# A decoder layer on one core: the sample's state taken up after a group's convolution, stores by ScalarE's queue, keys in four tiles, values in strips

## The chip, the core and the metric

The kernel runs on one core of a Trainium2 chip. The time is that of one launch on the device, in microseconds (us); lower is better. TensorE (PE) multiplies matrices, VectorE (DVE) and ScalarE (ACT) work on tiles, GpSimd (POOL) does a few small things here, and transfers are issued on the queues of SyncE (SP), POOL and ScalarE. Each engine, and each queue, takes its instructions strictly in order.

## What is computed

One step of a hybrid decoder layer for a prompt of 256 tokens and, with the same weights, 8 samples of one token each. All 264 columns go through every projection together. In short:

```python
h = rmsnorm(x) * norm_mix
q, k, v, z, xbc, dt, qm, gates = split(h @ w_in)
A = swa(q, k, v)               # window 128, 16 heads, sinks; samples see cache_swa_k/v
B = ssd(conv(xbc), z, dt)      # 4 groups of 8 heads; samples update state_ssm, state_conv
M = mem_attend(qm, k_mem, v_mem)   # 256 tokens: from mem_prompt, or cache_mem_k/v for samples
x = x + (sig(gA)*(A@w_up_swa) + sig(gB)*(B@w_up_ssd) + sig(gM)*(M@w_up_mem)) @ w_out
x = x + (silu(h2 @ w_gate) * (h2 @ w_up)) @ w_down      # h2 = rmsnorm(x)
```

Outputs are x of both kinds, the new keys and values, the SSD states and the last rows of the convolution. Of the sample's state, `s_ssm` (8 x 32 x 64 x 128 floats), every number is read, decayed, added to and written back.

## The kernel before

**Weights.** Every product is made in three matmuls of a 128x128 weight block (high part times high part, high times low, low times high). The weights stream in units: a unit is 512 KB, loaded on SP's queue into one of four `raw` tiles, split by ScalarE into `hi` (line 181) and by DVE into `lo` (line 182), up to three units ahead, and used by PE in 24 matmuls of 264 columns (line 160). Units are listed by hand in the order of the work: 32 for the keys and values of the memory (`pmem`), then those of `w_in` in groups of 8 units (`pin`), the three up projections (`pua`, `pum`, `pus`), `pout`, and the feed-forward part (`pg`, `pu`, `pdn`). A group ends with an `after` that empties four PSUM tiles; there are five PSUM tiles for this, so the next group starts as they come free.

**Side work.** All else is written as Python generators that are stepped once after each unit. `Side` holds a list of tasks and a credit: each unit adds 1.0 (list `side`) or 0.75 (list `slow`), a `yield n` spends n, and a `yield None` sets the credit to zero, that is, ends the step. A task may name what has to be ready first. In list `side` stand the norm of the memory (`mem_norm`), x's norm (`prep_x`), constants, the prompt's memory attention (`mem_prompt_work`), the window attention (`swa_keys`, `swa`), and per group of the SSD the convolution (V), the chunks (X) and the norm (N). In list `slow` stand the samples' memory attention, keys (`mem_sample_work`) and values (`mem_sample_values`), and the samples' state (`ssd_sample_work`, Y). The position in the program that comes out of this is a wish: a planner inside the framework, with a model of the times, fixes the order of each engine's instructions at build time.

**Start.** SP's queue loads the first quarters of `mem_prompt`, two small vectors into `vg` (lines 205, 206), then the first raw unit. PE turns `mem_prompt` into features (`mem_feats`, lines 308 to 318), three pairs ahead of the first unit's matmuls. ScalarE squares `mem_prompt` for its norm at line 327.

**Values of the memory for samples** (lines 726 to 749). For each sample and each half of the tokens: a tile of 1024 values, four matmuls (one for each head) of 256 columns into the four strips of 32 PSUM rows, with weights that are zero but for one column. Keys and values come through `ahead`, which keeps `depth` loads going, into two `lm` tiles.

**State of the samples** (lines 1280 to 1298). 32 pieces of four samples and two heads each. A piece is loaded on POOL's queue (line 591) into one of four slots of `ring`; ScalarE multiplies it four times (line 1294), DVE adds and reduces it (lines 1295, 1296), and POOL's queue stores it (line 1297). `ssd_sample_work(g)` may begin when `ssd_chunk_work(g)` has ended (line 1246).

**Stores.** Results go out on POOL's queue, those that ScalarE writes last too: om (line 691), v_tok (787), the last rows of the convolution (1047, 1049), so (1206) and sg (1399).

Of the kernel before, what the change touches and what calls it, by code (L numbers as in the profile page):

```python
# [77 lines left out]
def tile_hybrid_decoder_step(  # L78
# [80 lines left out]
    def mm(out, lhsT, rhs, start=True, stop=True):  # L159
        nc.tensor.matmul(out, lhsT=lhsT, rhs=rhs, start=start, stop=stop)  # L160
# [18 lines left out]
    def split(hi, lo, src):  # L179

        act(hi, src, AF.Copy)  # L181
        V.tensor_tensor(lo, src, hi.bitcast(F32), op=ALU.subtract)  # L182

# [18 lines left out]

    for t in range(2):
        load_mem(t, 0, 0)
    nc.sync.dma_start(vg[0:16], norm_mem[0].rearrange("(c p) -> c p", p=P))
    nc.sync.dma_start(vg[16:32], norm_mix[0].rearrange("(c p) -> c p", p=P))
# [45 lines left out]
    def do_split(n):  # L252
# [10 lines left out]
        else:  # L263
            split(hi, lo, raw)
# [8 lines left out]
    def group(name, loads, nk, xh, xl, after, perm=False, before=None):  # L273
# [145 lines left out]
    def prep_x():  # L419
# [4 lines left out]
        for h in range(2):  # L424
            for t in range(2):
# [3 lines left out]
                yield 1.3  # L429
# [129 lines left out]
    def h_group(col, after, perm=False, before=None):  # L559
        group("pin", w_loads(w_in[0], col), KT, hh, hl, after, perm, before)  # L560
# [34 lines left out]
    mem_loads = ahead([(None, c[0, b, mc * P:(mc + 1) * P].rearrange("m h d -> m (h d)"))  # L595
                       for c in (cache_mem_k, cache_mem_v) for b in range(NS) for mc in range(2)], lm, 2)
# [3 lines left out]
                         for j in range(16) for b in (0, 4)], lambda _: piece(512), 4)  # L600


    def mem_prompt_work():
# [50 lines left out]
        for hp in range(2):  # L654
            den = tiny("den", 4)
            pT = [t2("pT").rearrange("p (mc t) -> p mc t", mc=2) for _ in range(2)]
            for tb in range(2):
# [15 lines left out]
                for h in range(2):  # L673
                    V.tensor_scalar(pm[:, h], pm[:, h], den[:, 2 * tb + h:2 * tb + h + 1], None, op0=ALU.mult)
                p2 = sps("pmT").rearrange("p (h mc t) -> p h mc t", h=2, mc=2)
# [5 lines left out]
                yield 2.2  # L681
            for h in range(2):
# [8 lines left out]
                nc.gpsimd.dma_start(m_d[:, 2 * hd:2 * hd + 2, 0:NP], om)  # L691
                yield 0.2
        slow.ready.add("q")
    def mem_sample_work():
# [3 lines left out]
        for b in range(NS):  # L698
            qb = t4("qb")[:, 0:1024]
            nc.gpsimd.dma_start(qb, qd[b:b + 1].broadcast_to([P, 1024]))  # L700
            for mc in range(2):
                kc = next(mem_loads)
# [23 lines left out]
    def mem_sample_values():  # L726
        pT = mT["p"]
# [12 lines left out]
        o = t1("omsb")[:, 0:256]  # L740
        V.tensor_copy(o, po[:, 0:256])
        ps = sps("omT")
        for d in range(2):
            tr(ps[:, d * P:(d + 1) * P], o[:, d * P:(d + 1) * P])
        o = tiny("omsT", 64)
        V.tensor_copy(o.rearrange("p (h d b) -> p d h b", h=4, d=2),
                      ps[:, 0:256].rearrange("p (d h e) -> p d h e", d=2, h=4)[:, :, :, 0:NS])
# [23 lines left out]
    def swa_keys():  # L771
# [15 lines left out]
        nc.gpsimd.dma_start(p_swa_v[0, 0].rearrange("t h d -> t (h d)"), v_tok[:, 1])  # L787
# [33 lines left out]
    def swa():  # L821
# [37 lines left out]
        for a in range(2):  # L859
# [6 lines left out]
            yield 1.0  # L866
# [809 lines left out]
```

## Time and profile before

| What | us |
| --- | --- |
| Median of three runs | 1933.8 |
| Lowest and highest run | 1928.26, 1938.96 |
| The profiled execution | 1933.54 |
| Its span, first to last instruction | 1931.8 |
| PE busy | 1905.2 (99%) |
| DVE busy | 1168.0 (60%) |
| ACT busy | 969.7 (50%) |

PE's busy time counts any moment in which a matmul is in the array. A matmul of 264 columns is in it for some 285 ns, while the next starts 0.12 us after it, so a busy PE can still have lost a little at each change between kinds of matmul; only its idle time is a wait. The other engines' busy time matters where PE waits for one of them.

### The profile page before, as it was taken

Reading aid. Unit: us, or ns where it says so; the run is one execution under the profiler, and the core shown is the slowest. Engines: PE = TensorE matmul, PEld = TensorE weight load, DVE = VectorE, ACT = ScalarE, POOL = GpSimd, SP = SyncE. Lnnn points to the kernel's source line nnn. Section 1 sums busy time; section 2 is a strip of 40 time slices with the busy share of each in tenths; the row PEclk is TensorE's granted clock in tenths of the full one; section 3 lists DMA queues with packets and bytes.
Section 4 is the critical chain, followed back from the end, with each engine's and each line's share of the span. In section 5 each row is a group of like instructions: output and inputs, shape, how many; then the busy total and the mean of one; then the engine's idle time right before and its main releaser. Section 6 shows DMA issues by size and latency. Waiting matters only on the chain.

```text
span 1931.8 us, 37682 instructions
## 1 busy us (share of the span) xinstructions
PE 1905.2 (99%) x15401; PEld 1857.1 (96%) x15401; DVE 1168.0 (60%) x2246; ACT 969.7 (50%) x1423; POOL 133.6 (7%) x269
## 2 busy tenths in 40 slices
PE   8999999999999999999999999999999999999998
PEld 6899999989999999999999999999999999999998
DVE  5665577665568878588455666555445555445553
ACT  6654456665657685646444444444334434334443
POOL 3010101001002122011000000000000000000000
PEclk9999999999999999999999999999999999999999
DMA  8686758767668789778656656665556665566653
GB/s 278 209 264 214 212 171 297 223 190 234 200 181 279 241 228 301 250 262 282 180 189 213 222 182 176 184 182 180 183 178 183 178 185 177 184 177 183 176 192 126
DMA packets 191956, 402.92 MB, mean 209 GB/s; under 512 B 13891, under 2 KB 16242, under 8 KB 191648
## 3 DMA queue, kind: packets, MB, share of 16 engines
q1 hardware_dynamic: 169856, 324.13, 54.6%
q0 software_dynamic: 21776, 76.33, 11.9%
q8 instruction: 120, 1.97, 0.4%
q14 instruction: 52, 0.43, 0.1%
q10 hardware_dynamic: 152, 0.07, 0.0%
HBM read 376.53 MB, written 26.22 MB: 208 GB/s over the span
## 4 chain that ended last, share of the span: by engine, by line
PE 87%; DMA 4%; issue 4%; DVE 3%; ACT 2%; POOL 1%; ACTq 0%; SPq 0%; POOLq 0%; DVEq 0%
PE pin L160 25%; PE pu L160 13%; PE pdn L160 13%; PE pg L160 13%; PE pus L160 5%; PE pout L160 5%; PE pmem L160 5%; DMA ring<-in_state_ssm_dram 2%; PE pum L160 1%; PE pua L160 1%; DVE lo L182 1%; DMA ld<-in_cache_mem_v_dram 1%; DVE ring L1295 1%; DMA ld<-in_cache_mem_k_dram 1%; ACT hi L181 0%
## 5 line engine op out<-in xcount | busy, mean ns | idle before, releaser
L182 DVE TENSOR_TENSOR lo<-raw,hi 128x1024 fp32r<-128x1024 f32 (+1 forms) x626 | 746.8, 1196 | 599.4 <-ACT hi L181 598.2
L181 ACT ACTIVATE hi<-raw 128x1024 fp32r<-128x1024 f32 (+1 forms) x626 | 646.0, 1036 | 835.0 <-PE pin L160 191.8
L160 PE MATMUL pin<-hh,hi 128*128 128x264 f32 x1728 | 489.3, 287 | 0.6 <-DVE sig L1439 0.5
L160 PE MATMUL pin<-hl,hi 128*128 128x264 f32 x1728 | 489.0, 286 | 0.0
L160 PE MATMUL pin<-hh,lo 128*128 128x264 f32 x1728 | 473.8, 285 | 1.8 <-DVE lo L182 1.8
L160 PEld LDWEIGHTS pin<-hh,hi 128*128 128x128 f32 x1728 | 325.4, 189 | 5.6 <-issue 3.6
L160 PEld LDWEIGHTS pin<-hl,hi 128*128 128x128 f32 x1728 | 325.5, 188 | 2.7 <-issue 2.4
L160 PEld LDWEIGHTS pin<-hh,lo 128*128 128x128 f32 x1728 | 317.3, 188 | 3.8 <-DVE lo L182 2.3
L160 PE MATMUL pdn<-fah,hi 128*128 128x264 f32 x704 | 199.7, 285 | 0.0
L160 PE MATMUL pdn<-fal,hi 128*128 128x264 f32 x704 | 199.4, 285 | 0.0
L160 PE MATMUL pu<-h2h,hi 128*128 128x264 f32 x704 | 199.4, 284 | 0.0
L160 PE MATMUL pu<-h2l,hi 128*128 128x264 f32 x704 | 199.3, 284 | 0.0
L160 PE MATMUL pg<-h2l,hi 128*128 128x264 f32 x704 | 199.1, 285 | 0.0
L160 PE MATMUL pg<-h2h,hi 128*128 128x264 f32 x704 | 198.4, 284 | 0.0
L160 PE MATMUL pdn<-fah,lo 128*128 128x264 f32 x704 | 197.0, 284 | 0.0
L160 PE MATMUL pu<-h2h,lo 128*128 128x264 f32 x704 | 196.6, 284 | 0.0
L160 PE MATMUL pg<-h2h,lo 128*128 128x264 f32 x704 | 196.1, 284 | 0.0
L160 PEld LDWEIGHTS pdn<-fah,hi 128*128 128x128 f32 x704 | 132.7, 189 | 0.1
L160 PEld LDWEIGHTS pu<-h2h,hi 128*128 128x128 f32 x704 | 132.7, 189 | 0.0
L160 PEld LDWEIGHTS pg<-h2h,hi 128*128 128x128 f32 x704 | 132.7, 188 | 0.0
L160 PEld LDWEIGHTS pdn<-fal,hi 128*128 128x128 f32 x704 | 132.6, 188 | 0.1
L160 PEld LDWEIGHTS pu<-h2l,hi 128*128 128x128 f32 x704 | 132.6, 188 | 0.0
(531 smaller groups left out, 2966.0 us busy)
## 6 DMA issues: line engine op xcount, KB each, us to landing
raw<-in_w_in_dram SPq DMA_DIRECT2D x218, 512.0 KB, 4.3
raw<-in_w_gate_dram SPq DMA_DIRECT2D x88, 512.0 KB, 3.7
raw<-in_w_up_dram SPq DMA_DIRECT2D x88, 512.0 KB, 3.9
raw<-in_w_down_dram SPq DMA_DIRECT2D x88, 512.0 KB, 4.2
raw<-in_w_mem_kv_dram SPq DMA_DIRECT2D x32, 512.0 KB, 4.5
raw<-in_w_up_ssd_dram SPq DMA_DIRECT2D x32, 512.0 KB, 4.2
raw<-in_w_out_dram SPq DMA_DIRECT2D x32, 512.0 KB, 4.4
ld<-in_cache_mem_k_dram POOLq DMA_DIRECT2D x16, 512.0 KB, 5.8
```

Of the source, the lines that this page charges most:

```text
L160: nc.tensor.matmul(out, lhsT=lhsT, rhs=rhs, start=start, stop=stop)
L181: act(hi, src, AF.Copy)
L182: V.tensor_tensor(lo, src, hi.bitcast(F32), op=ALU.subtract)
L1295: V.scalar_tensor_tensor(hb, bb[:, b], dx[:, b:b + 1], hb, op0=ALU.mult, op1=ALU.add)
```

## The change

1. **State.** `ssd_sample_work(g)` may begin when group g's convolution has ended (the line that marks it moves from the end of `ssd_chunk_work` to its second line). State loads run two pieces ahead instead of three, and a piece spends 2.5 of credit instead of 2.0.
2. **Stores.** om, v_tok, the rows of the convolution, so and sg are stored by ScalarE's queue. At the start, the two `vg` loads go by ScalarE's queue, ahead of `mem_prompt`.
3. **Keys of the memory** go into four tiles by turns (two `lm`, two halves of `ring`), three loads ahead; values have their own two `lm` tiles.
4. **Values in strips.** For a sample, one 32-column weight with its four heads' columns serves four matmuls of 512 columns, one for each half of the tokens and each half of the 1024 values; the four strips of PSUM rows are those four, and a reduction at the end picks the heads out and adds the halves of the tokens.
5. **Start.** The squares follow the first `hi` on ScalarE; the first unit waits for two pairs of features instead of three; `prep_x` may begin only after unit 8, and its four loads spend 0.4 each.
6. **Steps.** The prompt's memory attention ends a step between softmax and transposes; in the window attention the splits of k and q spend 0.3, a step ends ahead of the product with the values, whose parts spend 0.2.
7. **m.** The split of m is parted from its load and put in the middle of the last z group.

```diff
     def split(hi, lo, src):
-        act(hi, src, AF.Copy)
+        h = act(hi, src, AF.Copy)
         V.tensor_tensor(lo, src, hi.bitcast(F32), op=ALU.subtract)
+        return h
...
+    nc.scalar.dma_start(vg[0:16], norm_mem[0].rearrange("(c p) -> c p", p=P))
+    nc.scalar.dma_start(vg[16:32], norm_mix[0].rearrange("(c p) -> c p", p=P))
     for t in range(2):
         load_mem(t, 0, 0)
-    nc.sync.dma_start(vg[0:16], norm_mem[0].rearrange("(c p) -> c p", p=P))
-    nc.sync.dma_start(vg[16:32], norm_mix[0].rearrange("(c p) -> c p", p=P))
...
+                if middle and 2 * u == nk // 2:
+                    middle()
...
-                    act(junk[:, 0:256], mem_t[t, h][:, c * 256:(c + 1) * 256], AF.Square, accum_out=ssm_[:, o:o + 1])
+                    with tc.issue_after(state["first"].ins):
+                        act(junk[:, 0:256], mem_t[t, h][:, c * 256:(c + 1) * 256], AF.Square, accum_out=ssm_[:, o:o + 1])
...
-                    for f in ((0, 1, 2) if u == 0 else (u + 2,)):
+                    for f in ((0, 1) if u == 0 else (u + 1,)):
...
                 x_t[t, h] = m
-                yield 1.3
+                yield 0.4
...
-    mem_loads = ahead([(None, c[0, b, mc * P:(mc + 1) * P].rearrange("m h d -> m (h d)"))
-                       for c in (cache_mem_k, cache_mem_v) for b in range(NS) for mc in range(2)], lm, 2)
+    homes = [0]
+    def anywhere(name):
+        homes[0] += 1
+        return (lm if homes[0] % 2 else ld)(name)
+    memk_loads, memv_loads = (
+        ahead([(None, c[0, b, mc * P:(mc + 1) * P].rearrange("m h d -> m (h d)")) for b in range(NS) for mc in range(2)],
+              pool, depth) for c, pool, depth in ((cache_mem_k, anywhere, 3), (cache_mem_v, lm, 2)))
...
-                         for j in range(16) for b in (0, 4)], lambda _: piece(512), 4)
+                         for j in range(16) for b in (0, 4)], lambda _: piece(512), 3)
...
                     V.tensor_scalar(pm[:, h], pm[:, h], den[:, 2 * tb + h:2 * tb + h + 1], None, op0=ALU.mult)
+                yield None
                 p2 = sps("pmT").rearrange("p (h mc t) -> p h mc t", h=2, mc=2)
...
-                yield 2.2
+                yield None
...
-                nc.gpsimd.dma_start(m_d[:, 2 * hd:2 * hd + 2, 0:NP], om)
+                nc.scalar.dma_start(m_d[:, 2 * hd:2 * hd + 2, 0:NP], om)
...
     def mem_sample_values():
+        w = t2("pb").rearrange("p (mc b c) -> p mc b c", mc=2, b=NS)
+        V.memset(w.rearrange("p mc b c -> p (mc b c)"), 0.0)
+        for b in range(NS):
+            V.tensor_copy(w[:, :, b, 4 * b:4 * b + 4], pT[:, :, b])
         po = sps("oms")
         for b in range(NS):
-            w = t1("pb")[:, 0:256].rearrange("p (mc h e) -> p mc h e", mc=2, h=4)
-            V.memset(w.rearrange("p mc h e -> p (mc h e)"), 0.0)
-            V.tensor_copy(w[:, :, :, b], pT.rearrange("p (mc b h) -> p mc b h", mc=2, b=NS)[:, :, b])
-            for mc in range(2):
-                vc = next(mem_loads)
-                for h in range(4):
-                    mm(po[32 * h:32 * h + 32, 0:256], w[:, mc, h], vc[:, h * 256:(h + 1) * 256],
-                       start=b == 0 and mc == 0, stop=b == NS - 1 and mc == 1)
-                yield 1.5
+            vc = [next(memv_loads) for _ in range(2)]
+            for mc, e in ((1, 0), (1, 1), (0, 0), (0, 1)):
+                o = 64 * mc + 32 * e
+                tc.keep_in_program_order(mm(po[o:o + 32, 0:512], w[:, mc, b], vc[mc][:, 512 * e:512 * e + 512],
+                                            start=b == 0, stop=b == NS - 1))
+            yield 3.0
...
+        for h in range(4):
+            V.tensor_reduce(o.rearrange("p (h d b) -> p h d b", h=4, d=2)[:, h], v[:, h % 2, h // 2, h], axis=AX.X, op=ALU.add)
...
             V.tensor_copy(kl[other], kl[own])
-            yield 1.0
+            yield 0.3
...
                 V.tensor_tensor(d[other], src, d[own].bitcast(F32), op=ALU.subtract)
-                yield 0.8
+                yield 0.3
...
+                yield None
                 po = sps("po")
...
-                        yield 0.4
+                        yield 0.2
...
         V.tensor_copy(ssd["xsS"][:, 4 * g:4 * g + 4], xs[:, :, NP:NT])
+        slow.ready.add(f"y{g}")
...
         ssd[f"y{g}"] = y
-        slow.ready.add(f"y{g}")
...
                 nc.gpsimd.dma_start(s_ssm[0, b0:b0 + 4, 2 * j:2 * j + 2].rearrange("b h p n -> (h p) b n"), h)
-                yield 2.0
+                yield 2.5
...
         nc.gpsimd.dma_start(mT["l"], m_d)
+
+    def split_m():
         for c in range(0, 8, 4):
...
-    z_group(3, load_m)
+    z_group(3, load_m, split_m)
...
-    side.add("x", prep_x())
+    side.add("x", prep_x(), ["go"])
...
             side.drain("m")
+            side.ready.add("go")
```

More of the change, by code (lines that the diff above doesn't have):

```diff
@@ L159, in mm @@
     def mm(out, lhsT, rhs, start=True, stop=True):
-        nc.tensor.matmul(out, lhsT=lhsT, rhs=rhs, start=start, stop=stop)
+        return nc.tensor.matmul(out, lhsT=lhsT, rhs=rhs, start=start, stop=stop)
     def tr(out, in_):
@@ L263, in do_split @@
         else:
-            split(hi, lo, raw)
+            h = split(hi, lo, raw)
+            if n == 0:
+                state["first"] = h
         parts[n] = (hi, lo)
@@ L271, in std_loads, with group @@
         return f
-    def group(name, loads, nk, xh, xl, after, perm=False, before=None):
+    def group(name, loads, nk, xh, xl, after, perm=False, before=None, middle=None):
         st = {}
@@ L555, in move_rows, with h_group @@
             tc.keep_in_program_order(nc.gpsimd.dma_start(to, of))
-    def h_group(col, after, perm=False, before=None):
-        group("pin", w_loads(w_in[0], col), KT, hh, hl, after, perm, before)
+    def h_group(col, after, perm=False, before=None, middle=None):
+        group("pin", w_loads(w_in[0], col), KT, hh, hl, after, perm, before, middle)
     qt = {}
@@ L701, in mem_sample_work @@
             for mc in range(2):
-                kc = next(mem_loads)
+                kc = next(memk_loads)
                 jk = t1("jks")
@@ L786, in swa_keys @@
         V.tensor_copy(v_new, kvt[:, 2:4, NP:NT])
[L787 removed]
+        nc.scalar.dma_start(p_swa_v[0, 0].rearrange("t h d -> t (h d)"), v_tok[:, 1])
         ks = t2("ks")[0:NS].rearrange("p (s c) -> p s c", s=2)
@@ L1326, in x_group, with z_group @@
         h_group(C_X + 512 * g, after_xbc(f"x{g}"), before=lambda: side.drain(XDRAIN[g]))
-    def z_group(g, before=None):
+    def z_group(g, before=None, middle=None):
         def f(ps):
@@ L1334, in f @@
             side.ready.add(f"z{g}")
-        h_group(C_Z + 512 * g, f, before=before)
+        h_group(C_Z + 512 * g, f, before=before, middle=middle)
     def dt_group():
```

21 lines of the change are left out of this document (10 added, 11 removed).

## The prediction

> **What bounds the kernel now.** I read the stretches first. Each row gives start and end, length, busy time (and instructions) of PE, PEld, DVE, ACT and POOL, then the granted clock, the DMA engines' busy share and GB/s.
>
> ```profile
> 0.00:11.90 11.90, 2.47 (x10) 1.92 (x10) 1.25 (x7) 3.86 (x8) 7.15 (x20) 1.00 0.80 194
> 11.90:112.00 100.10, 100.10 (x461) 81.43 (x461) 70.92 (x160) 68.11 (x146) 15.12 (x72) 1.00 0.78 258
> 112.00:455.00 343.00, 340.27 (x2754) 323.32 (x2753) 218.22 (x526) 185.82 (x315) 30.70 (x57) 1.00 0.70 219
> 455.00:580.00 125.00, 123.02 (x1083) 116.78 (x1083) 80.68 (x183) 80.81 (x133) 13.43 (x22) 1.00 0.69 209
> 580.00:760.00 180.00, 172.72 (x1479) 168.89 (x1479) 148.35 (x438) 121.85 (x216) 39.85 (x56) 0.99 0.85 255
> 760.00:1931.80 1171.80, 1166.66 (x9623) 1164.75 (x9621) 648.58 (x937) 509.28 (x610) 27.33 (x44) 1.00 0.62 194
> sum 1931.80, PE 1905.24 PEld 1857.10 DVE 1168.01 ACT 969.74 POOL 133.59; mean PE 317.54 PEld 309.52 DVE 194.67 ACT 161.62 POOL 22.27
> ```
>
> PE is the bound. It is idle for 1931.80 - 1905.24 = 26.6 us: 9.4 before the first weights arrive, none to 112 us, then 2.7, 2.0 and 7.3, and 5.1 after 760 us, nearly all of it the last stores. So no change of order can gain much over the middle 12 us plus a part of the start; only less work on PE itself could add to that. PE's own waits say who caused them (total, times, longest):
>
> ```profile
> PE pv L164 <- DMA vg<-in_norm_mix_dram: 7.0, 1, 7.0
> PE pua L160 <- ACT sig L1434: 3.8, 2, 2.6
> PE memT L164 <- DMA ring<-in_mem_prompt_dram: 2.5, 1, 2.5
> PE pin L160 <- DVE lo L182: 1.8, 2, 1.0
> PE pmT L164 <- DVE pm L674: 1.7, 2, 1.3
> PE oms L160 <- DMA ld<-in_cache_mem_v_dram: 1.6, 1, 1.6
> PE xtok L164 <- ACT xs L1037: 1.2, 1, 1.2
> PE pua L160 <- ACT hi L181: 0.8, 1, 0.8
> ```
>
> The largest of the middle is the up projection of the window branch (pua), which waits for ScalarE to empty the gates' PSUM (sig). ScalarE's timeline shows why sig was late both times:
>
> ```profile
> 614.13 1.28 ACT L1294 ACTIVATE ring<-ring,dsc 128x128 f32<-128x128 f32 x4 [3.37 <-DMA ring<-in_state_ssm_dram]
> 615.32 0.64 ACT L1434 ACTIVATE sig<-pin 128x264 f32<-128x264 f32 x2
> ...
> 753.25 0.69 ACT L1294 ACTIVATE ring<-ring,dsc 128x128 f32<-128x128 f32 x2 [2.88 <-DMA ring<-in_state_ssm_dram]
> 753.85 0.37 ACT L1434 ACTIVATE sig<-pin 128x264 f32<-128x264 f32 x1
> ```
>
> A piece of the sample's state had not landed, ScalarE stood 3.37 and 2.88 us at the head of its queue, and sig was next in line. The chain of waits holds the second load, and the stretch around it shows a lowered clock (0.96) and DMA engines that are busy throughout (0.98):
>
> ```profile
> 742.78 10.45 DMA ring<-in_state_ssm_dram
> ```
>
> ```profile
> 734.10:772.70 38.60, 35.15 (x274) 34.73 (x273) 29.39 (x87) 25.50 (x51) 11.30 (x17) 0.96 0.98 306
> ```
>
> State loads are issued on POOL's queue, which runs in order. What it stands waiting for, and how often ScalarE waits for a state load:
>
> ```profile
> POOL out_dram L1297 <- DVE ring L1295: 92.1, 16, 44.1
> POOL out_dram L1206 <- ACT so L1205: 54.9, 3, 26.4
> ...
> ACT ring L1294 <- DMA ring<-in_state_ssm_dram: 18.9, 12, 3.4
> ```
>
> **The change part by part.** The sum is made against the profiled execution's own 1933.5 us (span 1931.8 and 1.7 around it), which is the median of the runs, 1933.8, within noise.
>
> *State of the sample (E).* With four ring slots and loads three pieces ahead, the load for piece n+3 goes into the slot of piece n-1, whose store has just been queued; POOL stands until that store is through. Two pieces ahead, the slot's store is a whole piece older. A piece now has 2.5/0.75 = 3.3 units instead of 2.0/0.75 = 2.7, and a unit is 24 matmuls at 0.12 us (rows of PE below), 2.9 us. So the lead is 2 x 9.7 = 19.5 us against a landing of up to 10.45. The group's state starts after its convolution, some 13 units (38 us) before the place it has now, so the slower pace ends no later. Hence I expect the two waits for sig (3.8) and the one for hi beside them (0.8, in the same burst) to go: -4.6. What lies next, DVE's lo (1.8) and ScalarE's xs (1.2), I leave. The clock's dip follows the stall: 38.6 x 0.04 = 1.5 us, which goes with it. E = -4.6 - 1.5 = -6.1; at best the stretch's whole 7.3 and the dip, -8.8; at worst see the third rival.
>
> *ScalarE's results by its own queue (F).* 16 stores (4 om, 1 v_tok, 3 of the convolution's last rows, 4 so, 4 sg) leave POOL, where so alone held the queue 54.9 us. Each costs ScalarE's queue an issue:
>
> ```profile
> 476.07 0.53 ACTq L1084 DMA_DIRECT2D bc_d<-bcrows  x1
> ```
>
> 16 x 0.53 = 8.5 us, behind which hi splits and PSUM copies are queued. ScalarE has 58 of 180 us free in its fullest stretch and splits run up to three units ahead, so I cost it at 0. Without that cover: 18.9 us of ScalarE's waits cost PE 3.8, a fifth, so 8.5 would cost 1.7. Below zero lies only what E counts already.
>
> *Start (A).* The first raw weights' issue is behind the two vg loads on SP:
>
> ```profile
> 1.73 0.42 SPq L205 DMA_DIRECT2D vg<-in_norm_mem_dram  x1
> 2.20 0.42 SPq L206 DMA_DIRECT2D vg<-in_norm_mix_dram  x1
> 2.66 0.42 SPq L244 DMA_DIRECT2D raw<-in_w_mem_kv_dram  x1
> ...
> 10.81 1.06 ACT L181 ACTIVATE hi<-raw 128x1024 fp32r<-128x1024 f32 x1 [2.02 <-DMA raw<-in_w_mem_kv_dram]
> ```
>
> They move to ScalarE's queue, idle then; raw is issued 2.66 - 1.73 = 0.93 us earlier. The first hi waits for its landing, 8 us after the issue, in a stretch with the engines 0.80 busy, so not all of the 0.93 arrives: A = -0.5, ends 0 and -0.93. The squares that now follow the first hi fall into 11.9 to 112 us, where ScalarE is busy 68 of 100 and PE has no idle time; the features made one step later, and x's loads after unit 8 with shorter steps, lie in the same stretch. All 0: there is nothing to gain, and the 32 free us are the cover.
>
> *Prompt's memory attention, keys (B).* A step of nothing now lies between the softmax and its transposes, and keys come three ahead in four tiles, so DVE, which serves both, stands less for them. The wait for pm goes: B = -1.7, ends -1.7 and 0.
>
> *Window attention (C).* The q and k splits are given 0.3 of a step each instead of 0.8 and 1.0, which packs DVE's work closer:
>
> ```profile
> L874 DVE TENSOR_TENSOR qst<-qT,qst 64x1024 fp32r<-64x1024 f32 x4 | 4.9, 1217 | 0.1
> ```
>
> One of the two lo waits (1.0) lies behind these. 4.9 us of them within 6 x 0.3 = 1.8 units (5.2 us), beside two lo of 1.2 each, is a backlog of some 2 us; lo is made up to three units ahead, so C = 0, ends -1.0 (the wait vanishes) and +2 (the backlog shows).
>
> *Values in strips (D).* 64 matmuls of 256 columns in four strips, in 16 rounds, become 32 of 512 columns in 8 rounds. The columns streamed are the same; the rounds between full-width matmuls are halved.
>
> ```profile
> L160 PE MATMUL oms<-ld,pb 128*32 128x256 f32 x128 | 10.2, 389 | 1.6 <-DMA ld<-in_cache_mem_v_dram 1.6
> ```
>
> ```profile
> 161.56 0.28 PE L160 MATMUL pin<-hl,hi 128*128 128x264 f32 x1
> 161.68 0.28 PE L160 MATMUL pin<-hh,lo 128*128 128x264 f32 x1
> 161.89 0.62 PE L160 MATMUL ssq<-sqm,ones 128*32 128x256 f32 x2
> 162.44 0.39 PE L160 MATMUL pin<-hh,hi 128*128 128x264 f32 x1
> 162.67 0.28 PE L160 MATMUL pin<-hl,hi 128*128 128x264 f32 x1
> ```
>
> Nearest row for such a round: a strip matmul among full ones. Full ones start 0.12 apart; into the strip it is 0.21 and out of it 0.23, 0.2 us too much in all. 8 rounds fewer: -1.6, ends 0 and half of 10.2, -5.1. Both tiles of a sample are now needed at once and there are two tiles, so the next pair is loaded only when the round is over; a round has 4 units (11.7 us) for it. I take half of today's 1.6 wait as gone: -0.8, ends -1.6 and the fourth rival's. D = -2.4.
>
> The load and split of m are parted: PE's idle time after 760 us is the tail, so 0. With the split in the middle of the last z group, 4 units (11.7 us) remain before it is used.
>
> Sum: A -0.5, B -1.7, C 0, D -2.4, E -6.1, F 0 = **-10.7: 1922.8 us.**
>
> **Rivals.** *Second: the loads are late because the engines are full.* For it: a share of 0.98 and 306 GB/s where the load took 10.45 us; only the wait at 615 lay in a less loaded place. Then the second sig wait (2.6), hi (0.8) and the dip (1.5) stay: 1922.8 + 4.9 = 1927.7. Against it: the slower pace spreads the same bytes. The Trainium skill ("DMA: Bandwidth & Descriptors", "Issuing engines are not separate DMA queues") states this rule: transfers from ScalarE, SP or GpSimd run on the same 16 engines, and issuing from several saves only the issuing time. By that rule, the sum would be this rival's; the 0.98 agrees with it, while POOL's 54.9 us behind so speaks for the queue.
>
> *Third, the slower side: two ahead is too short a lead.* Place: ScalarE at L1294, with hi and sig behind it. POOL stands up to 44.1 us for DVE in front of a load; the lead is 19.5. If each of the 32 pieces kept ScalarE 3.4 us, today's longest, that is 109 us, of which a fifth (3.8 of 18.9) reaches PE: 22, 18 more than now. With A, B and D (-4.6): 1933.5 - 4.6 + 18 = 1947. It passes +0.5% from 2.9 us a piece on. Against it: only 12 of 32 wait now.
>
> *Fourth: values wait in each round.* PE runs in order; 7 rounds of 1.6 us make 11.2: 1922.8 + 0.8 + 11.2 = 1935. Against it: one wait in 16 rounds now, with the same two tiles.
>
> *Fifth: it doesn't do what it says.* A planner sets the order of instructions; if the pieces run where they ran, only A, B and D remain: 1929.
>
> **How the numbers follow.** 0.5% of 1933.8 is 9.7 us, about what a measurement of this kernel can tell from no change: faster means under 1924.1, slower over 1943.5. Forecast 0.60, second 0.17, third 0.11, fourth 0.06, fifth 0.06. The forecast's point is only 1.3 us under the line, but its unknowns lean down (D to -5.1, E to -8.8), so I give 0.48 of its 0.60 to faster and 0.12 to the middle. Same: 0.12 + 0.17 + 0.06 + 0.06 = 0.41; slower 0.11. Range: low, all lower ends together, -0.9 - 1.7 - 1.0 - 6.7 - 8.8 = -19.1, or 1914; high, past the fourth rival with C's +2, 1937. The third is left out, with a little below.
>
> **What would show it.** Right: no sig wait of PE; ScalarE's waits for state loads under 10 us; the stretch from 580 to 760 with under 3 us idle and a clock of 1.00; oms in 8 rounds with under 10.2 us; the first hi before 10.6. Wrong: ScalarE's waits for state loads above 18.9 us, PE waiting for values in several rounds, or PE waiting for lo during the q splits.

## The result, and the profile after

The changed kernel takes 1922.22 us (median of 6 runs, 1921.54 to 1925.11), the one before 1932.66 on the same chip (6 runs, 1928.26 to 1938.96): a ratio of 0.9949, with an interval of 0.9929 to 0.9969. The profiled run of the changed kernel happens to be its slowest, 1925.11 us with a span of 1923.4.

The same stretches as before, in the view by windows (start and end, length, busy time and instructions of PE, PEld, DVE, ACT and POOL, granted clock, DMA share, GB/s):

```profile
0.00:11.90 11.90, 5.66 (x19) 4.57 (x20) 3.97 (x11) 5.81 (x14) 8.83 (x23) 1.00 0.76 235
11.90:112.00 100.10, 97.60 (x453) 79.30 (x451) 69.17 (x157) 66.81 (x139) 12.53 (x69) 0.98 0.78 254
112.00:455.00 343.00, 341.68 (x2744) 325.66 (x2743) 219.53 (x530) 186.95 (x318) 25.63 (x48) 1.00 0.69 218
455.00:580.00 125.00, 124.39 (x1063) 117.48 (x1061) 93.22 (x256) 89.05 (x156) 21.35 (x32) 1.00 0.79 246
580.00:760.00 180.00, 176.16 (x1532) 173.03 (x1531) 140.57 (x370) 118.98 (x203) 33.08 (x48) 1.00 0.82 250
760.00:1923.40 1163.40, 1157.49 (x9541) 1154.94 (x9539) 642.50 (x922) 501.42 (x594) 20.94 (x34) 1.00 0.62 193
sum 1923.40, PE 1902.99 PEld 1854.99 DVE 1168.95 ACT 969.03 POOL 122.36; mean PE 317.16 PEld 309.17 DVE 194.83 ACT 161.51 POOL 20.39
```

PE's idle time has gone from 26.6 to 20.4 us: 3.2 less at the start, 2.5 more in the next stretch, then 1.4, 1.4 and 3.4 less in the three middle ones, 0.8 more behind them. The lowered clock has moved from the stretch at 734 to the one that begins at 11.9.

The view of the waits, PE's first, then the rows of ScalarE and POOL that belong to the state (total, times, longest):

```profile
PE pv L164 <- DMA vg<-in_norm_mix_dram: 5.2, 1, 5.2
PE memT L164 <- DMA mem<-in_mem_prompt_dram: 2.5, 1, 2.5
PE pst L160 <- DVE xw L1218: 1.3, 2, 1.1
PE pua L160 <- ACT hi L181: 1.2, 1, 1.2
PE pin L160 <- DVE lo L182: 1.2, 2, 0.7
...
PE pmT L164 <- DVE pm L688: 0.8, 1, 0.8
...
ACT ring L1315 <- DMA ring<-in_state_ssm_dram: 23.1, 16, 2.8
...
POOL ring L597 <- DVE s L1317: 79.4, 13, 23.4
...
POOL out_dram L1318 <- DVE ring L1316: 71.1, 16, 42.1
```

The waits for sig (3.8) and for the values (1.6) are gone, and that for pm has halved. But ScalarE's waits for the state's loads, which were to fall below 10 us, have risen from 18.9 to 23.1. That is the prediction's own sign of being wrong. So the loads do not land in time, and yet PE pays less for it. ScalarE's timeline, and one row of PE's, show how, at the two places where PE waited for sig before:

```profile
610.51 0.37 ACT L1457 ACTIVATE sig<-pin 128x264 f32<-128x264 f32 x1
...
614.76 1.08 ACT L1458 ACTIVATE sig<-sig 128x1056 f32<-128x1056 f32 x1
618.11 1.28 ACT L1315 ACTIVATE ring<-ring,dsc 128x128 f32<-128x128 f32 x4 [1.32 <-DVE lo L182]
...
739.89 2.65 ACT L1315 ACTIVATE ring<-ring,dsc 128x128 f32<-128x128 f32 x8 [1.87 <-DMA ring<-in_state_ssm_dram]
...
743.54 0.39 PE L160 MATMUL pua<-aTh,hi 128*128 128x264 f32 x1 [1.25 <-ACT hi L181]
```

At the first place a late piece stood straight ahead of sig (614.13 ahead of 615.32); now the gates' copies run without one, and the next piece starts 2.3 us behind the end of their last step. At the second two pieces still stand ahead of hi and sig, with a wait of 1.87 us for the load where it was 2.88; PE loses 1.25 for hi and nothing for sig.

### The profile page after: what moved, and what is told of

It is laid out like the page before. It is cut to its first block, busy times and chain, and to the rows that moved or that the text cites. A ratio compares the mean times of both kernels' runs of the same rounds, so it can differ in the third digit from the quotient of the medians.

```text
span 1923.4 us, 37545 instructions
## 1 busy us (share of the span) xinstructions
PE 1903.0 (99%) x15339; PEld 1855.0 (96%) x15339; DVE 1169.0 (61%) x2242; ACT 969.0 (50%) x1421; POOL 122.4 (6%) x253
## 3 DMA queue, kind: packets, MB, share of 16 engines
q8 instruction: 120, 1.97, 0.4%
## 4 chain that ended last, share of the span: by engine, by line
PE 89%; DMA 5%; issue 2%; DVE 2%; ACT 1%; POOL 0%; ACTq 0%; SPq 0%; POOLq 0%; DVEq 0%
PE pin L160 28%; PE pu L160 13%; PE pdn L160 13%; PE pg L160 13%; PE pus L160 5%; PE pout L160 5%; PE pmem L160 4%; PE pua L160 1%; DMA ring<-in_state_ssm_dram 1%; DMA mem<-in_mem_prompt_dram 1%; DMA out_dram<-ring 1%; DVE lo L182 1%; ACT hi L181 1%; DMA raw<-in_w_in_dram 1%; PE py L160 0%
```

## The experiments

In the table, PE's idle time is the span less PE's busy time, and the last but one column is half the length of the stretches for which the records show a granted clock of 0.5, without the one behind PE's last matmul (how these look is shown under E7 and E9). The ratio is to the kernel before, run on the same chip in turns; it differs by up to 0.001 from the quotient of the two medians. The median of the kernel before was 1930.72 for E1 to E4, 1929.66 for E5 to E8 and 1928.93 for E9 to E12.

| Kernel | Median us | Ratio, interval | Span profiled | PE idle | Lost at half clock | ScalarE for state loads |
| --- | --- | --- | --- | --- | --- | --- |
| before | 1932.66 | | 1931.8 | 26.6 | 1.7 | 18.9 |
| changed | 1922.22 | 0.9949, 0.9929–0.9969 | 1923.4 | 20.4 | 1.7 | 23.1 |
| E1, state undone | 1937.86 | 1.0031, 1.0016–1.0045 | 1937.8 | 28.6 | 8.5 | 20.5 |
| E2, state alone | 1940.89 | 1.0053, 1.0038–1.0068 | 1938.5 | 32.5 | 1.7 | 27.7 |
| E3, values undone | 1931.13 | 1.0000, 0.9983–1.0016 | 1937.1 | 27.8 | 5.1 | 22.7 |
| E4, stores undone | 1926.09 | 0.9975, 0.9965–0.9985 | 1924.2 | 19.9 | 3.4 | 18.7 |
| E5, three ahead | 1925.60 | 0.9969, 0.9951–0.9986 | 1922.9 | 19.4 | 1.7 | 20.0 |
| E6, begun late | 1939.51 | 1.0042, 1.0021–1.0063 | 1937.3 | 29.7 | 6.8 | 31.8 |
| E7, 2.0 a piece | 1936.93 | 1.0036, 1.0024–1.0048 | 1938.8 | 30.5 | 8.5 | 28.7 |
| E8, 2.6 a piece | 1929.54 | 0.9995, 0.9983–1.0007 | 1923.7 | 20.1 | 1.7 | 25.1 |
| E9, old steps | 1944.23 | 1.0069, 1.0053–1.0086 | 1941.8 | 34.1 | 1.7 | 38.9 |
| E10, state and stores alone | 1943.94 | 1.0073, 1.0058–1.0088 | 1943.3 | 34.4 | 3.4 | 27.3 |
| E11, one ahead | 1920.44 | 0.9955, 0.9941–0.9970 | 1917.8 | 16.7 | 0.0 | 20.8 |
| E12, x held back | 1926.77 | 0.9990, 0.9977–1.0003 | 1923.3 | 21.9 | 0.0 | 22.2 |

Idle time and half clock together account for the spans. From E11, the best of them, to E6 it is 13.0 idle and 6.8 of clock, 19.8, where the span is 19.5 longer; to the changed kernel 3.7 and 1.7, 5.4 of 5.6; to the kernel before 9.9 and 1.7, and 1.7 for the narrower rounds of the values (below), 13.3 of 14.0. The others agree within 2.7 us, but E9 is 4.9 us longer than its sum; that is left open.

The changed kernel, E5 and E11 have the same instructions in the same order on every engine (shown under E5 and E11). Their ratios, 0.9949, 0.9969 and 0.9955, are three measurements of one program, and so are their idle times, 20.4, 19.4 and 16.7 us. A difference of 0.2% or less from the changed kernel, or of up to 5.6 us between two profiled spans, is therefore no finding.

**E1: the state as it was, all else changed.** E2 is the opposite, the kernel before with the state part alone.

```diff
-                         for j in range(16) for b in (0, 4)], lambda _: piece(512), 3)
+                         for j in range(16) for b in (0, 4)], lambda _: piece(512), 4)
...
-        slow.ready.add(f"y{g}")
...
+        slow.ready.add(f"y{g}")
...
-                yield 2.5
+                yield 2.0
```

> The changed kernel with the state's part undone (begin after the chunks, three pieces ahead, 2.0 a piece). First theory (the state's part is worth about 5 us in the stretch 580 to 760, as predicted): 1927 to 1928 us, PE waits for sig there again. Rival (that gain came from the other parts, chiefly the stores that left POOL): 1921 to 1924 us, no sig wait.

> The kernel before with only the state's part. First theory: 1927 to 1928 us, about 5 less than before, and the sig waits gone. Rival (the other parts carry it): 1931 to 1933 us.

E1 gives 1.0031, E2 1.0053: both miss what was expected of them, 1927 to 1928 us, by some 10 us and more, and upwards. Beside the other parts the state part is worth 0.0031 + 0.0051 = 0.82%, nearly 16 us (0.62% against E5's measurement of the changed kernel); by itself it costs 0.53%, 10 us. A term of -6.1 that could be added to the others does not exist. PE's waits in E1, three rows of that view:

```profile
PE pst L160 <- DVE xw L1217: 4.6, 1, 4.6
PE pua L160 <- ACT sig L1457: 2.6, 2, 2.1
PE pin L160 <- DVE lo L182: 2.4, 1, 2.4
```

sig is waited for again, and lo as well, though ScalarE waits less for the state's loads (20.5) than in the changed kernel. The longer wait for sig (2.1, at 573 us) is not behind a piece: ScalarE had stood 3.0 us for a load of the chunks (dec), which is explained under E6. The largest has a cause of its own, which DVE's and PE's timeline of E1 show:

```profile
812.25 0.69 DVE L1217 TENSOR_TENSOR xw<-xdt,wf 128x512 f32<-128x512 f32 x1 [7.73 <-DMA out_dram<-rawT]
...
813.09 0.77 PE L160 MATMUL pst<-Btok,xw 128*128 128x128 f32 x2 [4.62 <-DVE xw L1217]
```

The tile that xw is written into held the convolution's last rows, and DVE stands 7.73 us until their store, now on ScalarE's queue, has landed; PE stands 4.62 behind it, and 6.8 us at half clock follow. DVE could go on 12.0 us after the last of these stores was issued (800.26 us); in the changed kernel it was 5.3, and the same wait of DVE is 1.0 us. That a store holds its tile until it has landed was no item of the prediction. E6 has the same wait (7.1 us of DVE, 4.0 of PE).

**E10: the state part with ScalarE's stores, without the rest.**

> The kernel before with the state part and ScalarE's stores alone. The state part alone gave a ratio of 1.005, undone in the changed kernel it gave 1.003, and the stores undone gave 0.9975 against 0.995. If the state part needs the stores moved off POOL's queue, so that its loads are issued earlier, this kernel is faster than the one before, ratio 0.995 to 0.999, and ScalarE's waits for state loads are under 15 us. If it needs the place that the other parts give to the work around it, the ratio stays at 1.001 to 1.006 and PE has small waits for lo, pmT, sig and hi, together 8 us or more.

The ratio is 1.0073, ScalarE's waits are 27.3 us, and PE waits 12.4 us for lo, pm, hi and sig: the stores do not make the state part good. It needs the keys, the steps, the values or the start, or several of them; which of these was not tried.

**E5 and E11: how far ahead the loads run.** The last argument is the number of loads that are under way.

```diff
-                         for j in range(16) for b in (0, 4)], lambda _: piece(512), 3)
+                         for j in range(16) for b in (0, 4)], lambda _: piece(512), 4)   # E5; 2 in E11
```

> The changed kernel with the state's loads three pieces ahead again, nothing else. First theory (two ahead keeps POOL from standing for a store, and that is what frees PE): 1926 to 1930 us, ScalarE's waits for state loads above 23 us. Rival (where the planner puts the pieces decides, and the depth does nothing by itself): 1921 to 1924 us.

> The changed kernel with state loads one piece ahead instead of two. The prediction's third rival at its strongest: ScalarE waits for nearly each of the 32 pieces, 60 us or more in all. By the prediction's exchange rate, a fifth of ScalarE's waits reaches PE: 37 us more of waits would cost 7 us, ratio 0.998 to 1.000. If what matters is only where a piece stands against the copies of the gates and the hi splits, and PE runs up to three units behind ScalarE, then the waits grow while PE's idle time grows by under 3 us: ratio 0.994 to 0.996.

E5 gives 0.9969, E11 0.9955, the changed kernel 0.9949; the intervals overlap. ScalarE's waits are 20.0, 20.8 and 23.1 us: no trend. The three traces show the reason: the number in the list moves nothing. On every engine the order of the instructions is the same in all three kernels, as the planner fixed it, and the state's first four loads go out together, one into each slot, with one ahead as with three. POOL's timeline of the changed kernel:

```profile
462.95 2.99 POOL L597 DMA_DIRECT2D ring<-in_state_ssm_dram  x4 [2.00 <-PE poS L160]
```

In E11 the same row of four starts at 460.49, in E5 at 462.63, and in the kernel before at 465.24. So neither run says what a shorter lead would do. What a load stands for, POOL's waits say. E11's rows, with ScalarE's:

```profile
ACT ring L1315 <- DMA ring<-in_state_ssm_dram: 20.8, 15, 3.2
...
POOL ring L597 <- DVE s L1317: 83.8, 14, 23.4
```

The loads stand on POOL's queue for DVE, which has still to read the slot (s, line 1317): 83.8 us in E11, 79.4 in the changed kernel, 84.4 in E5, ahead of 13 or 14 of the 32 loads. The depth in the list doesn't set when a load goes out; the four slots do. The loads themselves are as quick as they were. The page's list of DMA issues (KB each, median us from issue to landing) has the same row in the kernel before, in the changed one and in E11:

```profile
ring<-in_state_ssm_dram POOLq DMA_DIRECT2D x32, 256.0 KB, 5.5
```

**E6: the state begun after the chunks, as before. E7 and E8: 2.0 and 2.6 a piece.**

```diff
-        slow.ready.add(f"y{g}")       # E6: back to the end of ssd_chunk_work
...
-                yield 2.5
+                yield 2.0             # E7; 2.6 in E8
```

> The changed kernel with the state of a group begun after its chunks again, nothing else. First theory (the depth does it): 1921 to 1924 us. Rival (the early begin keeps the pieces from falling on the chunks and gates of later groups): 1930 to 1938 us, most of the loss of the run without the state's part, with single stalls of 2 us and more after 560 us, each followed by 3.4 us at half clock.

> The changed kernel with 2.0 a piece instead of 2.5. First theory (fewer pieces at a time on ScalarE and DVE): 1925 to 1929 us. Rival (pace means little once the begin is early): 1921 to 1924 us.

> A neighbour: the changed kernel with 2.6 a piece instead of 2.5, which by any theory of loads, queues or pace changes the time by less than 1 us: 1921 to 1924 us. Rival (each stall hangs on the exact order that the planner happens to make, so that neighbours differ by as much as the parts do): outside 1918 to 1928 us.

E6 gives 1.0042, E7 1.0036: each alone undoes the whole gain, against 0.9949 with both. ScalarE's waits rise to 31.8 and 28.7. In E7 a piece stands 4.67 us at the head of ScalarE's queue, and seven microseconds of other work, most of it the chunks', then hi and sig, wait behind it (ScalarE's timeline):

```profile
607.93 1.28 ACT L1315 ACTIVATE ring<-ring,dsc 128x128 f32<-128x128 f32 x4 [4.67 <-DMA ring<-in_state_ssm_dram]
...
616.49 1.05 ACT L181 ACTIVATE hi<-raw 128x1024 fp32r<-128x1024 f32 x1
...
617.44 0.94 ACT L1457 ACTIVATE sig<-pin 128x264 f32<-128x264 f32 x3
```

PE stood 2.47 us at 617, ahead of a product of the chunks, and the windows behind it show the second price of a stall, a clock of 0.50 for 3.4 us (and by the records again at 716, and for 6.8 us at 757):

```profile
613.70:617.10 3.40, 1.30 (x11) 1.09 (x9) 1.26 (x4) 3.37 (x8) 0.00 (x0) 1.00 0.24 92
617.10:620.50 3.40, 3.03 (x15) 2.73 (x16) 3.30 (x13) 3.38 (x7) 0.75 (x1) 0.50 0.45 101
```

The two largest stalls of E7 come later: 3.64 us at 715.6, for a square (sqy) that two pieces with waits of 5.24 and 2.15 stood ahead of, and 3.79 at 757.5, for a hi that itself waited 3.74 for its weights.

In E6 the second place is the one to look at (its timeline, ScalarE, then PE). A piece stands 3.93 us, a hi behind it 3.92 for its weights, PE 2.33 for that hi and 0.94 more for sig.

```profile
739.89 0.70 ACT L1315 ACTIVATE ring<-ring,dsc 128x128 f32<-128x128 f32 x2 [3.93 <-DMA ring<-in_state_ssm_dram]
...
749.36 1.06 ACT L181 ACTIVATE hi<-raw 128x1024 fp32r<-128x1024 f32 x1 [3.92 <-DMA raw<-in_w_up_swa_dram]
...
750.47 0.39 PE L160 MATMUL pua<-aTh,hi 128*128 128x264 f32 x1 [2.33 <-ACT hi L181]
```

Here, and at 757 us of E7, PE's wait ends with weights that landed late: between 700 and 760 us a weight load took up to 13.1 us from issue to landing in E6 and 12.8 in E7, at most 8.9 in the changed kernel. So not every stall is a matter of where a piece stands. But full DMA engines alone don't tell the two apart: between 740 and 760 us their share is 1.02 in E6, and in the changed kernel, which loses 1.25 us there, it is 1.02 too, with more bytes moved. The row of the changed kernel by windows, then that of E6:

```profile
740.00:760.00 20.00, 18.00 (x145) 17.58 (x145) 13.68 (x41) 15.94 (x33) 7.18 (x11) 1.00 1.02 331
```

```profile
740.00:760.00 20.00, 16.24 (x116) 15.61 (x116) 14.69 (x61) 13.19 (x27) 4.50 (x6) 0.91 1.02 274
```

E6 loses at 570 us too, by POOL's queue. POOL had stood 62.0 us for DVE, to store a piece, and issued that store, another one and only then the chunks' load of dec, at 557.44 us; in the changed kernel it went out at 552.66 and landed 3.8 us later, here 10.2 later. ScalarE stood 3.78 us for it, PE 1.68 for the hi behind it and 2.13 for sig, and 6.8 us at half clock follow. E1 has much the same at the same place: 61.8 us, issued at 557.08, landed 9.4 later.

E8, only 0.1 away from the changed kernel, gives 0.9995: 0.46% lost, or 0.26% against E5, the same program as the changed kernel in the same turns. Its profiled run, its fastest (1925.42), looks like the changed kernel's, so where its other runs lose is not seen.

**E3: the values in 16 rounds of 256 columns.** The old body of `mem_sample_values` stands in the changed kernel, with the new two tiles.

```diff
-            for mc, e in ((1, 0), (1, 1), (0, 0), (0, 1)):
-                o = 64 * mc + 32 * e
-                tc.keep_in_program_order(mm(po[o:o + 32, 0:512], w[:, mc, b], vc[mc][:, 512 * e:512 * e + 512],
-                                            start=b == 0, stop=b == NS - 1))
-            yield 3.0
+            for mc in range(2):
+                vc = next(memv_loads)
+                for h in range(4):
+                    mm(po[32 * h:32 * h + 32, 0:256], w[:, mc, h], vc[:, h * 256:(h + 1) * 256],
+                       start=b == 0 and mc == 0, stop=b == NS - 1 and mc == 1)
+                yield 1.5
```

> The changed kernel with the values in 16 rounds of 256 columns as before. Predicted term D: 1924 to 1925 us, 2.4 more than the changed kernel, PE's values at 10 us busy again. Rival (strips of 512 columns cost as much as they save): 1921 to 1923 us.

1931.13 us, ratio 1.0000, with runs from 1922.65 to 1939.2: some 6 us above what was expected, so more is lost than the rounds. The profiled run is the longest of the ten, and up to 491 us, where the rounds are all but over, it has lost only 1.6 us against the changed kernel by the starts of PE's groups. Then 7 us go in one place (its timeline, ScalarE, then PE):

```profile
499.33 2.44 ACT L1247 ACTIVATE dec<-dec,acs_tok 128x128 f32<-128x128 f32 x8 [7.24 <-DMA dec<-acs_d]
...
505.26 0.59 PE L160 MATMUL pin<-hh,hi 128*128 128x264 f32 x1 [5.43 <-ACT hi L181]
```

ScalarE stands 7.24 us for a row of the chunks that is spread over the partitions by a load, hi is behind it, PE stands 5.43, and 6.8 us at half clock follow. In the changed kernel that wait is 1.60.

**E4: the 16 stores on POOL's queue.**

```diff
-                nc.scalar.dma_start(m_d[:, 2 * hd:2 * hd + 2, 0:NP], om)
+                nc.gpsimd.dma_start(m_d[:, 2 * hd:2 * hd + 2, 0:NP], om)
...
```

> The changed kernel with the 16 stores back on POOL's queue (the two loads at the start stay on ScalarE's). First theory (term F is 0): 1921 to 1924 us. Rival (free POOL is what lets state loads go early): 1925 to 1928 us, with ScalarE's waits for state loads above 23 us.

0.9975: the stores are worth 0.26%, 5 us, by the changed kernel's own measurement, but 0.06% by E5's and 0.20% by E11's, and the intervals overlap: a gain is not shown. ScalarE's waits for the state are 18.7 us, not above 23, so the rival's reason is not there. In the profiled run 4.3 us are lost in one place by the starts of PE's groups, that of E3, here in E4's windows:

```profile
501.00:504.40 3.40, 1.63 (x10) 1.00 (x8) 1.51 (x2) 3.37 (x6) 0.00 (x0) 1.00 0.04 16
504.40:511.20 6.80, 6.73 (x28) 6.06 (x28) 5.00 (x14) 6.11 (x16) 0.77 (x1) 0.50 0.64 172
```

ScalarE stood 4.18 us for dec there. POOL issued the load at 491.75, in the changed kernel at 491.83, so it was not held up by a store on POOL's queue; it landed later. Why is not settled.

**E9: the steps of the two attentions as before, keys through two tiles.**

```diff
-               pool, depth) for c, pool, depth in ((cache_mem_k, anywhere, 3), (cache_mem_v, lm, 2)))
+               pool, depth) for c, pool, depth in ((cache_mem_k, lm, 2), (cache_mem_v, lm, 2)))
...
-                yield None
...
-                yield None
+                yield 2.2
...
-            yield 0.3
+            yield 1.0
...
-                yield 0.3
+                yield 0.8
...
-                yield None
...
-                        yield 0.2
+                        yield 0.4
```

> The changed kernel with the keys through two tiles and with the old steps of the prompt's memory attention and of the window attention (parts 3 and 6 undone); state, stores, values and start as changed. By the prediction's terms only B comes back: PE waits for pm again, 1.7 us, and the time is 1924 (ratio to the kernel before 0.996). The rival: parts of the change are not a sum, the steps move where the later pieces and copies land, and PE waits two or more times for 2 us or more after 500 us, each with 3.4 us at half clock behind it: 1930 or more (ratio 0.998 to 1.003), although nothing after 500 us was edited.

1.0069: with E10 the slowest of all, 1.2% from the changed kernel, and far from the 1.7 us that B was given. By E9's windows, PE is idle 7.25 us in the stretch of the attentions (1.3 in the changed kernel) and 9.5 between 580 and 760 (3.8), where nothing was edited:

```profile
112.00:455.00 343.00, 335.75 (x2675) 315.16 (x2674) 212.29 (x510) 184.22 (x309) 25.48 (x49) 1.00 0.70 220
...
580.00:760.00 180.00, 170.48 (x1464) 165.66 (x1463) 139.66 (x388) 115.84 (x193) 31.11 (x44) 1.00 0.79 235
```

Its waits are small ones, mostly of PE for DVE; only one behind 500 us is above 2 us, so the rival is right that the parts are not a sum, and not in how the time is lost:

```profile
PE pin L160 <- DVE lo L182: 6.9, 8, 2.1
...
PE pmT L164 <- DVE pm L688: 2.7, 2, 1.8
```

The kernel before, with these same steps, had only 2.7 us idle in that stretch. So it isn't the steps alone; some other part of the change needs the new ones, and which is not known. DVE is not short of time in E9 (212 of 343 us); we take it that it has its work in the wrong order for PE.

**E12: x's loads behind the first store of the memory's keys.**

```diff
+                state["km"] = nc.gpsimd.dma_start(
...
-                nc.gpsimd.dma_start(m, x_prompt[0, t * P:(t + 1) * P, h * 1024:(h + 1) * 1024])
+                with tc.issue_after(state["km"].ins):
+                    nc.gpsimd.dma_start(m, x_prompt[0, t * P:(t + 1) * P, h * 1024:(h + 1) * 1024])
```

> The changed kernel with x's four loads held back until the store of the first memory keys has been issued on POOL's queue. In the changed kernel x's loads are issued at 14.8 and 19.5 us, among the last parts of the prompt's memory, PE waits 2.5 us for one of those at 19.9 us, and the clock is at half for 3.4 us behind it (1.7 us lost). If x's loads make that wait, the wait and the half clock go and the kernel gains 2 to 4 us: ratio 0.993 to 0.994. If the raw weights' own loads make it, the wait stays at 2 to 3 us and the ratio is that of the changed kernel, 0.994 to 0.996.

The wait for mem_prompt falls to 1.2 us and the half clock at 20 us is gone, as the first theory has it. But E5 and E11, with x's loads where they were, wait 0.5 and 0.7 us for it and have no half clock there either, so the stall is one that the same program has in some executions, and E12 does not show that x's loads make it. The ratio is 0.9990, where E11 has 0.9955 in the same turns. The loads go out at 48.6 us, x's norm comes later on DVE and ScalarE, among the squares of the keys, and PE pays there (E12's timeline, POOL, then PE):

```profile
48.64 0.54 POOL L434 DMA_DIRECT2D ring<-in_x_prompt_dram  x1
...
92.54 0.74 PE L164 MATMUL kmT<-ident,km 128*128 128x128 f32 x4 [3.19 <-DVE km L388]
```

No version that was run beats the changed kernel by more than the measurement can tell.

## Why the prediction was right, and where it was not

**The sum** was -10.7; the medians differ by 10.4, the profiled executions by 8.4. Of these 8.4, 6.2 are PE's idle time and 1.7 the rounds of the values. But the sum came out right over a largest term whose reason fell, and other terms were off both ways; that 1922.8 lies 0.6 us from the median is in good part luck.

**E, the state (-6.1).** The step that failed is "the slot's store is a whole piece older ... the lead is 2 x 9.7 = 19.5 us against a landing of up to 10.45. Hence I expect the two waits for sig (3.8) and the one for hi beside them (0.8) to go." The waits for sig went, but the lead has no part in it: the number in the list moved no instruction (E5, E11), the first four loads go out together as before, and the loads are as late as they were (23.1 us of ScalarE's waits). Thirteen of the 32 stand behind DVE's reader of their slot. What the early begin and the pace do is to put the pieces and their stores elsewhere among the work of ScalarE and POOL, and each of the two is needed (E6, E7). That the place is what counts is read from the timelines; it was not tried by moving one piece alone, the gain at the second place is partly a shorter wait, and of E6's and E7's stalls there some end with weights that landed late. Nor was the idle time between 580 and 760 under 3 us, as "right" asked, but 3.8, and a wait for hi (1.2) is left.

**The dip of the clock (-1.5, in E).** "The clock's dip follows the stall" holds where there is a dip, and the one at 754 us went with its stall. But this profiled run has one at 20 us that the sum did not foresee, so the term brought nothing here. In E5's run of the same program the dip is at 745 us, and in E11's there is none.

**A, the start (-0.5, ends 0 and -0.93).** The first hi starts 3.3 us earlier, not 0.5 (the timeline of the changed kernel; SP's row is the issue of the first raw weights):

```profile
1.73 0.43 SPq L245 DMA_DIRECT2D raw<-in_w_mem_kv_dram  x1
...
7.47 1.05 ACT L181 ACTIVATE hi<-raw 128x1024 fp32r<-128x1024 f32 x1
...
19.85 0.47 PE L164 MATMUL memT<-ident,mem 128*128 128x128 f32 x1 [2.50 <-DMA mem<-in_mem_prompt_dram]
```

The issue moved by the 0.93 us that were counted; the landing moved by much more, probably since the first stretch's queues stand in another order; that was not tried. But nothing of it is left in this run at 40 us: PE waits 2.50 for the last part of mem_prompt and runs 3.4 us at half clock. In E9 and E11, with the same start and without a half clock there, the second group of pmem starts at 38.1 and 38.0 us, against 39.7 before: 1.6 to 1.8 us. By the first group of pin 0.8 and 1.1 of it are left (111.8 and 111.5 us against 112.6). The term was mis-sized, twice too small, and nothing of it arrives when the stall at 20 us comes.

**B, the prompt's memory attention (-1.7).** "The wait for pm goes" did not come true: it halves, 1.7 to 0.8 (1.2 in E5, 0.5 in E11). By the starts of PE's groups, the changed kernel gains 1.9 us from the first group of pin to the fifth, but E5's run of the same program only 0.5. So -1.7 was too much by the wait itself, and E9 says that it is not a term that stands alone.

**C, the window attention (0).** Between 270 and 380 us, where the splits of q are, the wait of 1.0 for lo is gone, and PE waits 0.6 for the last split of q instead (qst). That is -0.4, within the ends; no backlog of lo shows, and 0 was nearly right against the kernel before. What the steps save beside the other parts (E9) was not seen.

**D, the values (-1.6 and -0.8).** The view of the lines has the group's busy time and the mean of one:

```profile
L160 PE MATMUL oms<-ld,pb 128*32 128x512 f32 x64 | 8.5, 605 | 0.0
```

10.2 us have become 8.5, and the wait of 1.6 is gone: -3.3 by this row, where -2.4 was given. The mechanism is right, and both parts were somewhat larger. The 0.2 us of a round was read too low: it left out the time from the start of the strip's two matmuls to the next full one (161.89 to 162.44). Counted from the last full matmul ahead of a round to the second one behind it, the rounds take 2.5 us less in all, beside the wait.

**F, the stores (0).** E4 puts them between -1 and -5 us beside the rest, E10 against E2 at +0.2%, both within the intervals. So 0 is not refuted. It asked only what 16 issues cost ScalarE and what POOL's queue gains; the landings that others wait for (dec, rawT) were left out.

**The rivals.** The second (the engines are full): they are full from 740 to 760 us in the fast kernel as in the slow ones, the median landing is 5.5 us before and after, and the waits for sig went all the same; so what it states is there, and it did not decide between these two kernels. In E6 and E7 it has a share: the late weights. The Trainium skill ("DMA: Bandwidth & Descriptors", "Issuing engines are not separate DMA queues") says that issuing from several engines saves only the issuing time; the equal landings agree, and E4 shows no clear gain from the move either. The third (two ahead too short) did not come about, with 23.1 us of waits in all, but E11 does not test it, since its lead is the same. The fourth did not come about: no wait for values. The fifth (the pieces run where they ran) did not for the begin and the pace: the pieces run from 506 to 535 and from 581 to 875 us, before from 507 to 513 and from 588 to 897. For the depth it is just what happened.

## What to carry to other kernels

When an engine waits for a load, look first at what the load itself stood behind on its queue. A late load does no harm where nothing urgent stands behind the one who waits. Where instructions are placed by a planner, look in the trace whether an edit has moved an instruction at all; one that has not is a second measurement of the same program, and shows how far apart two of these lie. Parts of a change are not terms of a sum there: undo each part from the finished kernel and try it alone on the old one (here the same part saves 0.82% in the one and costs 0.53% on the other), and be wary of a gain that a step of 0.1 in one pace takes away. Price a stall of PE with the half clock that may follow it.

## What was not expected of the hardware

**A stall can cost a second time.** Stretches at a granted clock of 0.50, where a trace has any ahead of PE's last matmul, are 3.4 or 6.8 us long and begin at or right behind a stall. Each costs half its length: in the one at 20 us of the changed kernel pmem's matmuls start 0.42 us apart, behind it 0.23. They lie on a grid: in E7 they begin at 19.7, 617.1, 716.1 and 757.0 us, and the distances (597.3, 99.0, 41.0) are 175, 29 and 12 times 3.413. What counts seems to be how idle PE was within one step of that grid. E9 shows it twice, by windows laid on its grid:

```profile
729.50:732.90 3.40, 1.97 (x17) 1.75 (x15) 3.40 (x13) 1.06 (x1) 2.27 (x3) 1.00 0.78 258
732.90:736.30 3.40, 2.69 (x20) 2.58 (x21) 3.40 (x8) 0.00 (x0) 0.75 (x1) 1.00 0.75 198
862.60:866.00 3.40, 1.67 (x11) 1.46 (x12) 3.40 (x10) 0.00 (x0) 1.52 (x2) 1.00 0.99 356
866.00:869.40 3.40, 3.40 (x18) 3.40 (x17) 3.40 (x8) 0.00 (x0) 0.76 (x1) 0.50 1.03 396
```

A stall of 2.14 us at 733 fell on two steps, which stayed 1.97 and 2.69 us busy, and the clock stayed at 1.00; two stalls of 1.50 and 0.67 us left one step 1.67 busy, under half, and the next ran at 0.50. With the grid laid over all fourteen traces, from 12 us to PE's last matmul, each of the 17 steps with at most 1.58 us of busy PE was followed by half clock, and none with 1.80 or more that was not itself at half clock; between 1.60 and 1.76 both occur. The Trainium skill ("TensorE: Matmul & The Clock Gate", "Part 1: The HAM clock gate") describes such a window of 3413 ns that runs free of the kernel, and half rate behind an idle one; the grid agrees. In its section "Why this matters for your kernels" that page of the Trainium skill asks for no idle gaps of over some 3 us. Here the half busy step above was enough, and a gap of 3.19 us in E12, which fell on two steps, cost no half clock. So the same kernel can pay or escape by where its stall falls on the grid. The changed kernel, E5 and E11 are one program, and have half clock at 20 us, at 745 us and not at all; their stalls differ in length as well, so how much of the spread between runs comes from the grid is open.

**A store holds its tile.** 7.73 us of DVE for a store of a few rows (E1), 1.0 for the same store in the changed kernel, is a difference of landing: 12.0 and 5.3 us behind the last issue. What made it land late was not tried.
